# Quarter sums on GpSimd, a second gate and up block by seven products, and later tables, in a decoder trunk

## The chip, the cores and the metric

The kernel runs on one core of one Trainium2 chip. The metric is the device time of one execution in microseconds (us). Engines are named as in the profile: PE is TensorE (matmul), DVE is VectorE, ACT is ScalarE, POOL is GpSimd, SP is SyncE, which issues the weight DMAs.

## The reference

Two layers on a residual stream h of 256 tokens by 1024 channels, then an RMSNorm. All in float32:

```
for each layer:
  h = h + 1/2 * SwiGLU(RMSNorm(h))     # ffn1: gate and up 1024 x 2816, down 2816 x 1024
  u = RMSNorm(h); z = u @ W_in         # 5536 columns
  m = sum of three gated branches (latent attention, differential attention with ALiBi, trailing means)
  h = h + m @ W_out
  h = h + 1/2 * SwiGLU(RMSNorm(h))     # ffn2, same shapes
out = RMSNorm(h)
SwiGLU(x) = (silu(x @ W_gate) * (x @ W_up)) @ W_down
```

The change touches the four feed-forward stages (ffn1 and ffn2 of both layers) and the tables that attention reads: distances, mask, cosines and sines of the positions, and lambda.

## The kernel before, in words

**Products in three.** A float32 product is made of three matmuls. Each weight tile of 4 x 128 rows by 512 columns (1 MB, 128 partitions x 2048) is loaded by SP into a buffer `raw` (six of them), ACT casts it to `hi`, DVE subtracts `lo = raw - hi` (`wsplit_now` L182, `parts` L217; three buffers each of hi and lo), and PE adds hi*hi, hi*lo and lo*hi. For 256 tokens (two groups of 128) a tile is 24 matmuls of 512 columns.

**A feed-forward stage** (`ffn`, L492) goes over the 2816 columns in five blocks of 512 and a half block of 256. A block needs gate and up columns, 1024 by 1024 weights, four tiles. After a block, silu and a product make g, and in the next block PE transposes g and ACT and DVE split it into `ghi` and `glo` (`turned`). The down projection then has 22 groups of 128 rows in two halves of 512 columns.

**Seven products.** The fourth block (`SEVEN = 1536`) and the first eight row groups of the down projection are made as a two by two block product with seven instead of eight block products (Strassen and Winograd's scheme). Class `Seven` (L225) has these parts:

- `stream` (L235): sums of quarters of the activations: uf = hi + lo (2048 columns), four sums `sf` of 512 columns, then the split into `sh` (ACT) and `sl` (DVE).
- `sums` (L251): three of the four sums of weight quarters, 2048 columns each (t1 = b12 - b11, t2 = b22 - t1, b12 = b22 - b12). They stand at the start of the block before.
- `more` (L262): the splits p1 and p5, at the end of the block before.
- `run` (L280): products and splits in the order p1, p5, p2, p6, p3, p4, p7. The fourth sum, t1 = b21 - t2 (L297), overwrites t1 once p5 has been split from it. Each product is 12 matmuls.

`Down` (L317) does the same for the down projection. `open` makes the sums b11 - b12 and b22 - b12, `rest` (L345) two more, b22 - b11 and then that less b21, all by `minus` (L328, the subtraction itself is L329). Its products are mixed with ordinary tiles (`tiles`, L331).

**Buffers.** The large tiles (8 KB per partition) come from two sets: seven buffers of `big` (activations hi and lo, sh, sl, t2, ghi, gates and so on) and three of `big2` (uf, sf, t1, glo). A tile waits until one is free.

**Order.** Instructions are written in program order, and a scheduler gives each engine its own order by readiness in a cost model; waits follow from the tiles' reads and writes. On the chip each engine runs its list in order. `ahead()` (L175) begins the split of the first tile of the next block.

**Tables.** In layer 0, `table_loads` (L600) is called from the list `opening` (L1053), which is worked off between the first tiles: three small loads into `pi` and parts of a large tile `tables`. `tables()` (L611) is called at the start of the second block as `midway`.

Of the kernel before, what the change touches and what calls it, by code (L numbers as in the profile page):

```python
# [11 lines left out]
F32 = mybir.dt.float32  # L12
F32R = mybir.dt.float32r
I32 = mybir.dt.int32
BF16 = mybir.dt.bfloat16
AF = mybir.ActivationFunctionType
ALU = mybir.AluOpType
# [17 lines left out]

SEVEN = 1536

# [13 lines left out]
def plan():  # L51

    tiles = []

    def add(name, layer, k, nk, c, nc_):
        tiles.append((name, layer, k, nk, c, nc_))

    def ffn(layer, pre):
        for c in range(0, 2 * DFF, 1024):
            blocks = range(c, min(c + 1024, 2 * DFF), 512)  # L60
            order = [(b, k) for k in (0, 4) for b in blocks] if c == 0 else [(b, k) for b in blocks for k in (0, 4)]
            if c // 2 == SEVEN:
                order = [(c, 0), (c + 512, 0), (c + 512, 4), (c, 4)]
            for b, k in order:
                add(f"{pre}_gu", layer, k, 4, b, 512)
        for half in range(2):
            for k in range(0, KF, 4):
                add(f"{pre}_w_down", layer, k, min(4, KF - k), half * 512, 512)

    for l in range(DEPTH):  # L70
        ffn(l, "ffn1")
        for c, n in ((C_CQ, 416), (C_P, 512), (C_DQ, 512)):
            for k in (0, 4):
                add("w_in", l, k, 4, c, n)
        add("mla_w_uq", l, 0, 2, 0, 768)
        add("ukv", l, 0, 1, 0, 1024)
        for c in (C_DK, C_DV):
            for k in (0, 4):
                add("w_in", l, k, 4, c, 512)
        add("pool", l, 0, 4, 0, 128)  # L80
        for half in range(2):
            for i in range(3):
                for k in (0, 4):
                    add("w_in", l, k, 4, C_G + i * D + half * 512, 512)
        for half in range(2):
            for i in (2, 0, 1):
                add(f"w_branch{i}", l, 0, 4, half * 512, 512)
        for half in range(2):
            for k in (0, 4):
                add("w_out", l, k, 4, half * 512, 512)  # L90
        ffn(l, "ffn2")
    return tiles
# [3 lines left out]
def trunk(ctx, tc, x, xt, positions, wall, small, lamrow, fnorm, out):  # L96
# [128 lines left out]
    class Seven:  # L225
# [9 lines left out]
        def stream(self, uh, ul, place=big2):  # L235

            uf = big2([P, KD, S], F32, "uf")
            f = lambda a: a.rearrange("p k s -> p (k s)")
            nc.vector.tensor_tensor(out=f(uf), in0=f(uh).bitcast(F32), in1=f(ul).bitcast(F32), op=ALU.add)
            sf = place([P, 4, 4, P], F32, "sf")  # L240
            a = lambda i, j: uf[:, 4 * j:4 * j + 4, i * P:(i + 1) * P]
            for dst, x, y, op in ((0, a(1, 0), a(1, 1), ALU.add), (1, sf[:, 0], a(0, 0), ALU.subtract),
                                  (2, a(0, 0), a(1, 0), ALU.subtract), (3, a(0, 1), sf[:, 1], ALU.subtract)):
                nc.vector.tensor_tensor(out=sf[:, dst], in0=x, in1=y, op=op)
            self.sh = big([P, 4, 4, P], F32R, "sh")
            self.sl = big([P, 4, 4, P], F32R, "sl")
            g = lambda x: x.rearrange("p s k q -> p (s k q)")
            nc.scalar.copy(out=g(self.sh), in_=g(sf))
            nc.vector.tensor_tensor(out=g(self.sl), in0=g(sf), in1=g(self.sh).bitcast(F32), op=ALU.subtract)

        def sums(self, specs):  # L251

            s11, s12, s22, self.s21 = specs
            self.b12, self.b11, self.b22 = wraw(s12), wraw(s11), wraw(s22)
            self.t1 = big2([P, 4, 512], F32, "t1")
            self.t2 = big([P, 4, 512], F32, "t2")
            sub = lambda o, x, y: nc.vector.tensor_tensor(out=flat(o), in0=flat(x), in1=flat(y), op=ALU.subtract)
            sub(self.t1, self.b12, self.b11)
            sub(self.t2, self.b22, self.t1)
            sub(self.b12, self.b22, self.b12)  # L260
# [19 lines left out]
        def run(self, between):  # L280
# [15 lines left out]

            nc.vector.tensor_tensor(out=flat(self.t1), in0=flat(self.b21), in1=flat(self.t2), op=ALU.subtract)  # L297
            p3 = parts(self.b22)
# [18 lines left out]
    class Down(Seven):  # L317
# [10 lines left out]
        def minus(self, o, x, y):  # L328
            nc.vector.tensor_tensor(out=flat(o), in0=flat(x), in1=flat(y), op=ALU.subtract)  # L329

# [13 lines left out]

        def rest(self, ah, al, early):  # L345
            self.ah, self.al = ah, al
# [8 lines left out]
            early()  # L355
            self.tiles(0, [8])
            p5 = parts(self.b11)
            self.product(d, 0, p5)
# [3 lines left out]
            self.tiles(1, [8])  # L362
            b21 = wraw(self.spec(0, 4))
            p2 = parts(b21)
            self.product(a, (0, 1), p2, True)
            self.tiles(0, [12])
# [15 lines left out]
            add(u3, b, m1)  # L382
            add(m5, u3, m5)
            self.tiles(0, [20])
            for t, half, x in ((1, 0, u3), (0, 1, u2), (1, 1, m5)):
# [106 lines left out]
    def ffn(l, pre, u, following, midway=None):  # L492
# [19 lines left out]
        for c in range(0, DFF, 512):  # L512
            n = min(512, DFF - c)
            if c == 512 and midway:
                midway()
            spec = lambda b, k: (f"{pre}_gu", l, k, 4, b, 512)
            if c == 0:
# [13 lines left out]
                u.factor()  # L531
                seven = Seven(u.xh, u.xl)
                down = Down(lambda k: ghi[0][:, k, :], lambda k: glo[0][:, k, :])
            elif c == SEVEN:
                rows = seven.run(lambda: turned(*pending))
                ps = [[rows[t][m] for t in range(2)] for m in range(2)]
            elif n == 512:
                ps = []
                if c + 512 == SEVEN:
                    at = 2 * c + 1024  # L540
# [3 lines left out]
                for m in range(2):  # L544
                    ps.append(gemm_tokens([spec(2 * c + m * 512, k) for k in (0, 4)], u.xh, u.xl, 512))
                    if m == 0:
                        turned(*pending)
                        if c + 1024 == SEVEN:
                            seven.stream(u.hi, u.lo)
                        elif c == 2048:  # L550
                            down.stream(ghi[0], glo[0], big)
            else:
                both = gemm_tokens([spec(2 * c, k) for k in (0, 4)], u.xh, u.xl, 512, lambda: turned(*pending))
                ps = [[b[:, m * n:(m + 1) * n] for b in both] for m in range(2)]
            if c + 512 == SEVEN:
                seven.more()
            elif n < 512:
                down.open(lambda half, k: (f"{pre}_w_down", l, k, min(4, KF - k), half * 512, 512))
            elif c != SEVEN:
                ahead()  # L560
# [9 lines left out]
        nxt = following() if following else None  # L570
        down.rest(lambda k: ghi[k // 8][:, k % 8, :], lambda k: glo[k // 8][:, k % 8, :], lambda: turned(*pending))
        for half in range(2):
# [27 lines left out]
    def table_loads(after):  # L600

        tb["pi"] = pi = sp.tile([P, 2], I32, tag="pi", name="pi", bufs=1)
        tb["all"] = big([P, 8, S], F32, "tables")
        pr, lr = tb["all"][:, 4, :].bitcast(I32), tb["all"][:, 5, :]
        for dst in (pi, pr[:, :2], lr[:, :2].bitcast(I32)):
# [5 lines left out]
    def tables():  # L611
        pi, pr = tb["pi"], tb["all"][:, 4, :].bitcast(I32)

        part = tb["all"][:, 0:4, :].rearrange("p (t i) s -> p t i s", t=2)
        ci = sp.tile([P, 2, 2], I32, tag="ci", name="ci", bufs=1)
# [7 lines left out]
        for t in range(2):  # L623
            nc.vector.tensor_scalar(out=part[:, t, 0, :], in0=rf[:, 0, :], scalar1=cf[:, 0, t:t + 1], scalar2=4096.0,
                                    op0=ALU.subtract, op1=ALU.mult)
            nc.vector.tensor_scalar(out=part[:, t, 1, :], in0=rf[:, 1, :], scalar1=cf[:, 1, t:t + 1], scalar2=None,
                                    op0=ALU.subtract)
            nc.vector.tensor_tensor(out=part[:, t, 0, :], in0=part[:, t, 0, :], in1=part[:, t, 1, :], op=ALU.add)
            nc.vector.scalar_tensor_tensor(out=ndist[:, t, :], in0=part[:, t, 0, :], scalar=-1.0, in1=part[:, t, 0, :],
                                           op0=ALU.mult, op1=ALU.min)  # L630
            nc.gpsimd.affine_select(out=ndist[:, t, :], in_=ndist[:, t, :], compare_op=ALU.is_ge, fill=-1e33,
# [28 lines left out]

        lr = tb["all"][:, 5, :].rearrange("p (l f d) -> p l f d", l=DEPTH, f=4)
        lpr = tp.tile([P, DEPTH, 2, 32], F32, tag="C", name="lpr")
# [389 lines left out]
    opening += [lambda k=k: u.first(k) for k in range(4, KD)]  # L1052
    opening += [lambda: table_loads(u.hi[:, KD - 1, :2].bitcast(F32))] + [lambda: None] * 3  # L1053
    opening += [lambda t=t, n=n: nc.sync.dma_start(out=h[:, t, n * 512:(n + 1) * 512],
# [68 lines left out]
```

## Time and profile before

| what | value |
|---|---|
| median of 3 runs | 1208.63 us (1207.67 to 1209.4) |
| the profiled execution | 1207.28 us, span 1205.5 us |
| granted TensorE clock in it | 0.998 |
| ACT busy | 637.7 us, 53% of the span |
| SP weight loads of 1 MB | 182, median 4.9 us to landing |
| HBM read | 210.85 MB, 176 GB/s over the span |

A row of instructions names the line of the kernel, the engine, the operation, the tile written and the tiles read, the shape and the count, then busy time, the mean of one in ns, and the idle time in front of it with what ended it. A row of the timeline has the start, the duration, and in brackets the idle time before. A row of waits has the total, the number and the longest. A row of stretches has the length, then the busy time of each engine. A busy PE is not PE at its peak, since its matmuls overlap.

### The profile page before, as it was taken

The numbers are of one execution on the slowest core, as the hardware profiler recorded it, in microseconds if no ns is written. First come the engines' busy times: TensorE is split into PE (matmuls) and PEld (weight loads), VectorE is DVE, ScalarE is ACT, GpSimd is POOL, SyncE is SP. The second block draws the span as 40 slices with busy tenths as digits, with TensorE's granted clock in tenths as the row PEclk, the third lists the DMA queues.
The fourth block names the chain that finished last, engine by engine and source line by source line (L and its number), as shares of the span: only waits on it lengthen the run. The fifth ranks groups of instructions, "written<-read, shape, count | busy, mean of one in ns | idle before, by whom it ended". The sixth has DMA issues, their size and how long they took to land.

```text
span 1205.5 us, 14989 instructions
## 1 busy us (share of the span) xinstructions
PE 1186.7 (98%) x5896; PEld 991.4 (82%) x5896; DVE 923.0 (77%) x1200; ACT 637.7 (53%) x817; POOL 66.2 (5%) x127
## 2 busy tenths in 40 slices
PE   9989999999999999999999999999999999999997
PEld 7778888998788888888888888899977888888886
DVE  6889867777756757998757998768686486499876
ACT  5647446456544454655554655455465435546543
POOL 0000000700100000000000000025010000000000
PEclk9999999999999999999999999999999999999999
DMA  8846356336345454563764563653443554545540
GB/s 268 337 141 220 133 195 242 123 105 210 107 173 190 162 178 172 176 240 105 247 219 162 175 244 105 226 189 116 157 150 126 196 178 172 202 153 203 166 165 36
DMA packets 35478, 212.86 MB, mean 177 GB/s; under 512 B 4176, under 2 KB 5584, under 8 KB 12112
## 3 DMA queue, kind: packets, MB, share of 16 engines
q1 hardware_dynamic: 34272, 210.52, 50.2%
q10 hardware_dynamic: 1136, 1.40, 0.4%
q8 instruction: 46, 0.75, 0.2%
q14 instruction: 24, 0.20, 0.1%
HBM read 210.85 MB, written 1.05 MB: 176 GB/s over the span
## 4 chain that ended last, share of the span: by engine, by line
PE 88%; DVE 6%; issue 2%; ACT 2%; DMA 2%; POOL 0%; SPq 0%; POOLq 0%; ACTq 0%; DVEq 0%
PE acc L211 17%; PE acc L212 17%; PE acc L213 17%; PE acc L277 13%; PE acc L343 9%; PE e L343 3%; PE o L856 2%; DVE lo L194 2%; PE tr L502 1%; DMA raw<-wall 1%; PE tr L822 1%; PE tr L849 1%; PE tr L212 1%; PE tr L213 1%; PE tr L211 1%
## 5 line engine op out<-in xcount | busy, mean ns | idle before, releaser
L194 DVE TENSOR_TENSOR lo<-raw,hi 128x1024 fp32r<-128x1024 f32 (+3 forms) x258 | 392.1, 1535 | 151.5 <-ACT hi L193 150.8
L193 ACT CAST hi<-raw 128x1024 fp32r<-128x1024 f32 (+3 forms) x258 | 327.7, 1295 | 267.1 <-PE acc L213 135.9
L212 PE MATMUL acc<-lo,uhi 128*128 128x512 f32 (+1 forms) x768 | 300.0, 391 | 6.3 <-DVE lo L194 6.2
L211 PE MATMUL acc<-hi,uhi 128*128 128x512 f32 (+1 forms) x768 | 301.0, 393 | 0.9 <-DVE uhi L450 0.9
L213 PE MATMUL acc<-hi,ulo 128*128 128x512 f32 (+1 forms) x768 | 299.2, 390 | 0.9 <-DVE ulo L451 0.5
L212 PEld LDWEIGHTS acc<-lo,uhi 128*128 128x128 f32 x768 | 144.7, 188 | 36.5 <-DVE lo L194 8.1
L211 PEld LDWEIGHTS acc<-hi,uhi 128*128 128x128 f32 x768 | 144.3, 188 | 31.1 <-issue 2.6
L213 PEld LDWEIGHTS acc<-hi,ulo 128*128 128x128 f32 x768 | 144.6, 188 | 30.7 <-DVE ulo L451 1.1
L222 DVE TENSOR_TENSOR lo<-raw,hi 128x2048 fp32r<-128x2048 f32 x44 | 100.8, 2290 | 44.1 <-ACT hi L221 44.1
L221 ACT CAST hi<-raw 128x2048 fp32r<-128x2048 f32 x44 | 84.3, 1915 | 93.9 <-PE acc L213 36.1
L841 ACT ACTIVATE e<-e,mx 128x128 f32<-128x128 f32 (+1 forms) x96 | 42.7, 446 | 56.0 <-DVE mx L837 34.1
L343 PE MATMUL acc<-hi,ghi 128*128 128x512 f32 x168 | 66.3, 395 | 0.0
L343 PE MATMUL acc<-lo,ghi 128*128 128x512 f32 x168 | 65.7, 391 | 0.0
L343 PE MATMUL acc<-hi,glo 128*128 128x512 f32 x168 | 65.5, 391 | 0.0
L211 PE MATMUL acc<-uhi,hi 128*128 128x256 f32 x192 | 55.6, 290 | 0.0
L212 PE MATMUL acc<-ulo,hi 128*128 128x256 f32 x192 | 55.2, 288 | 0.0
L213 PE MATMUL acc<-uhi,lo 128*128 128x256 f32 x192 | 55.0, 288 | 0.0
L277 PE MATMUL acc<-hi,sl 128*128 128x512 f32 x128 | 49.8, 389 | 0.0
L277 PE MATMUL acc<-hi,sh 128*128 128x512 f32 x128 | 49.8, 389 | 0.0
L277 PE MATMUL acc<-lo,sh 128*128 128x512 f32 x128 | 49.8, 389 | 0.0
L416 POOL TENSOR_TENSOR r<-r,mhalf 128x2 f32<-128x2 f32 x6 | 4.2, 702 | 714.3 <-DVE r L415 714.3
L565 ACT ACTIVATE sg<-acc,r 128x512 f32<-128x512 f32 (+1 forms) x44 | 28.5, 653 | 27.7 <-PE acc L213 27.7
(258 smaller groups left out, 1968.2 us busy)
## 6 DMA issues: line engine op xcount, KB each, us to landing
raw<-wall SPq DMA_DIRECT2D x182, 1024.0 KB, 4.9
raw<-wall SPq DMA_DIRECT2D x26, 256.0 KB, 5.1
raw<-wall SPq DMA_DIRECT2D x10, 512.0 KB, 3.6
raw<-wall SPq DMA_DIRECT2D x4, 832.0 KB, 4.4
raw<-wall SPq DMA_DIRECT2D x2, 768.0 KB, 6.6
xT<-xt SPq DMA_DIRECT2D x8, 128.0 KB, 4.4
h<-x SPq DMA_DIRECT2D x4, 256.0 KB, 6.0
fn<-fnorm ACTq DMA_DIRECT2D x1, 512.0 KB, 4.2
```

The lines of the kernel that those rows point to most:

```text
L193: nc.scalar.copy(out=hif[:, ks], in_=rawf[:, ks])
L194: nc.vector.tensor_tensor(out=lof[:, ks], in0=rawf[:, ks], in1=hif[:, ks].bitcast(F32), op=ALU.subtract)
L211: nc.tensor.matmul(ps, lhsT=lh, rhs=rh, start=start, stop=False)
L212: nc.tensor.matmul(ps, lhsT=lh, rhs=rl, start=False, stop=False)
L213: nc.tensor.matmul(ps, lhsT=ll, rhs=rh, start=False, stop=stop)
L221: nc.scalar.copy(out=flat(hi), in_=flat(x))
L222: nc.vector.tensor_tensor(out=flat(lo), in0=flat(x), in1=flat(hi).bitcast(F32), op=ALU.subtract)
L277: nc.tensor.matmul(ps, lhsT=x, rhs=y, start=not onto and k == 0 and n == 0, stop=k == 3 and n == 2, skip_group_check=onto)
L343: nc.tensor.matmul(bank, lhsT=x, rhs=y, start=new and n == 0, stop=n == 2, skip_group_check=not new)
L565: nc.scalar.activation(out=sg, in_=ps[0][t], func=AF.Silu, scale=r)
L841: nc.scalar.activation(out=e[:, sl], in_=e[:, sl], func=AF.Exp, bias=mx[:, i:i + 1], scale=-(2.0 ** -(hd + 1)) if slope else -1.0, accum_o ...
L856: nc.tensor.matmul(o[:, hd * 64:(hd + 1) * 64], lhsT=eT[:, j * P:(j + 1) * P], rhs=v[:, kt, hd * 64:(hd + 1) * 64], start=(kt == 0), stop= ...
```

## The change

- All quarter sums go from DVE to POOL: uf and sf in `stream`, three in `sums`, the fourth in `run`, and `minus` in the down projection. The splits (`sl`, `lo`) stay on DVE.
- Two blocks of a stage are made by seven products, the third (column 1024) and the fifth (2048), in place of the fourth. The order of their weight tiles in memory follows. `stream` runs once, after the first block, and serves both.
- The down projection's `stream` moves from the fifth block to the start of the half block.
- In `rest`, b21's load, the split p2 and its product come ahead of p5.
- `table_loads` moves from the opening to the start of the third block of the first stage, with small tiles of its own; `tables()` moves into that stage's down projection, ahead of its last tile of the first half. A large tile is no longer needed for them.

```
-SEVEN = 1536
+SEVENS = 1024, 2048
...
-            if c // 2 == SEVEN:
+            if c // 2 in SEVENS:
                 order = [(c, 0), (c + 512, 0), (c + 512, 4), (c, 4)]
...
-            nc.vector.tensor_tensor(out=f(uf), in0=f(uh).bitcast(F32), in1=f(ul).bitcast(F32), op=ALU.add)
+            nc.gpsimd.tensor_tensor(out=f(uf), in0=f(uh).bitcast(F32), in1=f(ul).bitcast(F32), op=ALU.add)
...
-                nc.vector.tensor_tensor(out=sf[:, dst], in0=x, in1=y, op=op)
+                nc.gpsimd.tensor_tensor(out=sf[:, dst], in0=x, in1=y, op=op)
...
-            sub = lambda o, x, y: nc.vector.tensor_tensor(out=flat(o), in0=flat(x), in1=flat(y), op=ALU.subtract)
+            sub = lambda o, x, y: nc.gpsimd.tensor_tensor(out=flat(o), in0=flat(x), in1=flat(y), op=ALU.subtract)
...
-            nc.vector.tensor_tensor(out=flat(self.t1), in0=flat(self.b21), in1=flat(self.t2), op=ALU.subtract)
+            nc.gpsimd.tensor_tensor(out=flat(self.t1), in0=flat(self.b21), in1=flat(self.t2), op=ALU.subtract)
...
         def minus(self, o, x, y):
-            nc.vector.tensor_tensor(out=flat(o), in0=flat(x), in1=flat(y), op=ALU.subtract)
+            nc.gpsimd.tensor_tensor(out=flat(o), in0=flat(x), in1=flat(y), op=ALU.subtract)
...
-        def rest(self, ah, al, early):
+        def rest(self, ah, al, early, late):
...
             self.tiles(0, [8])
+            b21 = wraw(self.spec(0, 4))
+            p2 = parts(b21)
+            self.product(a, (0, 1), p2, True)
             p5 = parts(self.b11)
...
             self.tiles(1, [8])
-            b21 = wraw(self.spec(0, 4))
-            p2 = parts(b21)
-            self.product(a, (0, 1), p2, True)
             self.tiles(0, [12])
...
             add(m5, u3, m5)
+            late()
             self.tiles(0, [20])
...
-            if c == 512 and midway:
-                midway()
+            if c == 1024 and midway:
+                table_loads(g[0][:, :2])
...
                 seven = Seven(u.xh, u.xl)
+                seven.stream(u.hi, u.lo)
...
-                        if c + 1024 == SEVEN:
-                            seven.stream(u.hi, u.lo)
-                        elif c == 2048:
-                            down.stream(ghi[0], glo[0], big)
             else:
+                down.stream(ghi[0], glo[0], big)
                 both = gemm_tokens([spec(2 * c, k) for k in (0, 4)], u.xh, u.xl, 512, lambda: turned(*pending))
...
-        tb["all"] = big([P, 8, S], F32, "tables")
-        pr, lr = tb["all"][:, 4, :].bitcast(I32), tb["all"][:, 5, :]
+        tb["pr"] = pr = sp.tile([P, S], I32, tag="pr", name="pr", bufs=1)
+        tb["lr"] = lr = sp.tile([P, DEPTH * P], F32, tag="lr", name="lr", bufs=1)
...
-    opening += [lambda: table_loads(u.hi[:, KD - 1, :2].bitcast(F32))] + [lambda: None] * 3
+    opening += [lambda: None] * 4
```

`tables()` computes the same values, with its partial distances in `ndist` and a small tile instead of the large one.

More of the change, by code (lines that the diff above doesn't have):

```diff
@@ L532, in ffn @@
                 seven = Seven(u.xh, u.xl)
+                seven.stream(u.hi, u.lo)
                 down = Down(lambda k: ghi[0][:, k, :], lambda k: glo[0][:, k, :])
-            elif c == SEVEN:
+            elif c in SEVENS:
                 rows = seven.run(lambda: turned(*pending))
@@ L538, in ffn @@
                 ps = []
-                if c + 512 == SEVEN:
+                if c + 512 in SEVENS:
                     at = 2 * c + 1024
@@ L547, in ffn @@
                         turned(*pending)
-                        if c + 1024 == SEVEN:
-                            seven.stream(u.hi, u.lo)
-                        elif c == 2048:
-                            down.stream(ghi[0], glo[0], big)
             else:
+                down.stream(ghi[0], glo[0], big)
                 both = gemm_tokens([spec(2 * c, k) for k in (0, 4)], u.xh, u.xl, 512, lambda: turned(*pending))
                 ps = [[b[:, m * n:(m + 1) * n] for b in both] for m in range(2)]
-            if c + 512 == SEVEN:
+            if c + 512 in SEVENS:
                 seven.more()
@@ L558, in ffn @@
                 down.open(lambda half, k: (f"{pre}_w_down", l, k, min(4, KF - k), half * 512, 512))
-            elif c != SEVEN:
+            elif c not in SEVENS:
                 ahead()
@@ L570, in ffn @@
         nxt = following() if following else None
-        down.rest(lambda k: ghi[k // 8][:, k % 8, :], lambda k: glo[k // 8][:, k % 8, :], lambda: turned(*pending))
+        down.rest(lambda k: ghi[k // 8][:, k % 8, :], lambda k: glo[k // 8][:, k % 8, :], lambda: turned(*pending),
+                  midway or (lambda: None))
         for half in range(2):
@@ L611, in tables @@
     def tables():
-        pi, pr = tb["pi"], tb["all"][:, 4, :].bitcast(I32)
-        part = tb["all"][:, 0:4, :].rearrange("p (t i) s -> p t i s", t=2)
+        pi, pr = tb["pi"], tb["pr"]
         ci = sp.tile([P, 2, 2], I32, tag="ci", name="ci", bufs=1)
@@ L623, in tables @@
         for t in range(2):
-            nc.vector.tensor_scalar(out=part[:, t, 0, :], in0=rf[:, 0, :], scalar1=cf[:, 0, t:t + 1], scalar2=4096.0,
+            nd, part = ndist[:, t, :], tp.tile([P, S], F32, tag="C", name="part")
+            nc.vector.tensor_scalar(out=nd, in0=rf[:, 0, :], scalar1=cf[:, 0, t:t + 1], scalar2=4096.0,
                                     op0=ALU.subtract, op1=ALU.mult)
[L626 to L630, printed above, removed]
+            nc.vector.tensor_scalar(out=part, in0=rf[:, 1, :], scalar1=cf[:, 1, t:t + 1], scalar2=None, op0=ALU.subtract)
+            nc.vector.tensor_tensor(out=nd, in0=nd, in1=part, op=ALU.add)
+            nc.vector.scalar_tensor_tensor(out=nd, in0=nd, scalar=-1.0, in1=nd, op0=ALU.mult, op1=ALU.min)
             nc.gpsimd.affine_select(out=ndist[:, t, :], in_=ndist[:, t, :], compare_op=ALU.is_ge, fill=-1e33,
@@ L659, in tables @@
         nc.vector.tensor_scalar(out=cosq, in0=cosk, scalar1=MLA_SCALE, scalar2=None, op0=ALU.mult)
-        lr = tb["all"][:, 5, :].rearrange("p (l f d) -> p l f d", l=DEPTH, f=4)
+        lr = tb["lr"].rearrange("p (l f d) -> p l f d", l=DEPTH, f=4)
         lpr = tp.tile([P, DEPTH, 2, 32], F32, tag="C", name="lpr")
```

## Prediction

> **What bounds the kernel now.** I read the page first, then the waits of TensorE (PE), then the chain.
>
> ```profile
> span 1205.5 us, 14989 instructions
> PE 1186.7 (98%) x5896; PEld 991.4 (82%) x5896; DVE 923.0 (77%) x1200; ACT 637.7 (53%) x817; POOL 66.2 (5%) x127
> PE 88%; DVE 6%; issue 2%; ACT 2%; DMA 2%; POOL 0%; SPq 0%; POOLq 0%; ACTq 0%; DVEq 0%
> ```
> ```profile
> PE acc L212 <- DVE lo L194: 6.2, 3, 3.7
> ```
> ```profile
> 139.00 2.72 PE acc L277 x12
> 164.28 2.72 PE acc L277 x12
> 175.16 5.44 PE acc L343 x24
> ```
>
> PE carries 88% of the chain and loses almost nothing to anyone: its largest wait, for the subtraction that makes the low part of a split weight tile, is 6.2 us in all. The chain also gives the true price of a matmul of 512 columns: 12 follow each other in 2.72 us, so 0.227 us each (the 0.39 us of a single one overlaps its neighbours). A kernel in this state gets faster if PE issues fewer matmuls and the others keep up. So the second question is how near VectorE (DVE) is to not keeping up. I cut one steady feed-forward stage, the second of layer 0, into stretches:
>
> ```profile
> core 0: us, PE busy (x) PEld busy (x) DVE busy (x) ACT busy (x) POOL busy (x), PEclk, DMA share, GB/s
> 449.30:471.10 21.80, 21.80 (x102) 18.12 (x101) 15.42 (x14) 9.90 (x8) 0.00 (x0) 1.00 0.57 193
> 471.10:494.80 23.70, 23.70 (x110) 19.74 (x109) 23.08 (x15) 11.72 (x9) 0.00 (x0) 1.00 0.51 175
> 494.80:514.75 19.95, 19.95 (x93) 16.60 (x93) 19.11 (x14) 15.95 (x12) 0.00 (x0) 1.00 0.47 153
> 514.75:537.50 22.75, 22.75 (x106) 18.90 (x106) 22.08 (x19) 12.42 (x11) 0.00 (x0) 1.00 0.71 244
> 537.50:560.80 23.30, 23.30 (x109) 19.18 (x108) 19.74 (x14) 12.27 (x11) 0.00 (x0) 1.00 0.28 92
> 560.80:608.00 47.20, 47.20 (x213) 38.78 (x213) 33.85 (x26) 24.65 (x21) 0.00 (x0) 1.00 0.68 241
> ```
>
> These are the second gate and up block, the third, the fourth by seven products (the run), the fifth, the half block with the head of the down projection, and the rest. PE is busy without a gap. DVE is full in the third to the fifth: 19.11 of 19.95 us in the run. DVE keeps up with very little room. In the run the room per tile is small as well:
>
> ```profile
> 494.83 1.92 ACT L221 CAST hi<-raw 128x2048 fp32r<-128x2048 f32 x1 [3.52 <-PE acc L213]
> 503.69 2.29 DVE L222 TENSOR_TENSOR lo<-raw,hi 128x2048 fp32r<-128x2048 f32 x1 [0.20 <-ACT hi L221]
> ```
>
> A split may begin when PE has finished with the tile three before it (three buffers; the cast waits for PE). It takes 1.92 + 2.29 = 4.2 us, and PE has two products, 5.44 us, to do meanwhile. The slack is 1.2 us.
>
> **The change part by part.** *Fewer matmuls.* A block by four tiles is 96 matmuls, by seven products 84. One more such block per stage saves 12 x 0.227 = 2.72 us, in four stages 10.9 us, all on the path.
>
> *Work off DVE.* One stage of before:
>
> ```profile
> L329 DVE TENSOR_TENSOR raw<-raw 128x2048 f32<-128x2048 f32 x4 | 9.2, 2290 | 0.1
> L257 DVE TENSOR_TENSOR t<-raw,t 128x2048 f32<-128x2048 f32 x1 | 2.3, 2289 | 0.0
> L239 DVE TENSOR_TENSOR uf<-ghi,glo 128x2048 f32<-128x2048 f32 x1 | 2.3, 2281 | 0.0
> L297 DVE TENSOR_TENSOR t<-raw,t 128x2048 f32<-128x2048 f32 x1 | 2.3, 2282 | 0.0
> L244 DVE TENSOR_TENSOR sf<-uf 128x512 f32<-128x512 f32 x4 | 2.6, 686 | 0.0
> L486 DVE TENSOR_TENSOR glo<-tr,ghi 128x512 fp32r<-128x512 f32 x11 | 7.1, 684 | 0.0
> L282 DVE TENSOR_TENSOR u<-acc,m 128x512 f32<-128x512 f32 x1 | 0.7, 682 | 0.0
> ```
>
> Four L329, three L257 and one L297 are 8 x 2.29 = 18.3 us; two streams of one L239 and four L244 (0.69 us) are 10.1 us. DVE loses 28.4 us per stage and gains, for the second seven-product block, three splits (6.9) and five additions of 0.68 (3.4). Taken alone that is 18 us of relief.
>
> *The same work on GpSimd (POOL).* There it is 12 sums of 2048 columns (four per seven-product run, four in the down projection) and two streams. The trace has no POOL subtraction of that size; its own subtractions and additions bound it:
>
> ```profile
> 230.48 0.60 POOL L910 TENSOR_TENSOR pp<-pp 128x254 f32<-128x254 f32 x1
> 231.05 0.22 POOL L916 TENSOR_TENSOR pp<-pp 128x16 f32<-128x16 f32 x1
> 231.23 0.70 POOL L918 TENSOR_TENSOR pp<-pp 128x240 f32<-128x240 f32 x1
> 342.29 1.05 POOL L962 TENSOR_TENSOR o<-o,hs 128x512 f32<-128x512 f32 x1
> ```
>
> From L916 to L918, both subtractions, a column costs 0.48/224 = 2.14 ns, so 2048 columns about 4.55 us; from L916 to the addition L910 1.6 ns, so 3.45 us. I take 4.55, since the sums are subtractions, and 1.05 for a quarter of a stream (L962 has its size). A stage then has 12 x 4.55 + 2 x (4.55 + 4.2) = 72 us on POOL, of some 180. [...]
>
> *What POOL takes from DVE.* Two engines are free beside each other only if nothing is shared. These rows show that something is:
>
> ```profile
> 220.03 1.37 DVE L194 TENSOR_TENSOR lo<-raw,hi 128x1024 fp32r<-128x1024 f32 x1 [3.49 <-ACT hi L193]
> 221.99 1.21 DVE L194 TENSOR_TENSOR lo<-raw,hi 128x1024 fp32r<-128x1024 f32 x1
> 234.45 1.22 DVE L194 TENSOR_TENSOR lo<-raw,hi 128x1024 fp32r<-128x1024 f32 x1
> 342.60 2.96 DVE L194 TENSOR_TENSOR lo<-raw,hi 128x1024 fp32r<-128x1024 f32 x2 [2.11 <-ACT hi L193]
> ```
> ```profile
> 220.28 1.69 POOL L918 TENSOR_TENSOR pp<-pp 128x240 f32<-128x240 f32 x1
> 222.18 1.49 POOL L910 TENSOR_TENSOR pp<-pp 128x254 f32<-128x254 f32 x1
> ```
>
> POOL's L918 takes 1.69 instead of 0.70 when it begins behind a DVE split that ends at 221.40, and L910 1.49 instead of 0.60 beside the split of 221.99 to 223.20: each ends about 0.5 us after that split. The other way round, the two splits at 342.60 take 2.96 where two in a row take about 2.3, with the first 0.74 us inside POOL's L962. So a DVE subtraction with both inputs in SBUF and a POOL instruction exclude each other, and whoever comes second waits for the end of the other. No row shows it for a POOL instruction above 1.05 us at work. [...]
>
> *The sum by stretches.* I add what DVE keeps and what POOL holds, take off two thirds of DVE's operations that read PSUM (one SBUF input at most, so they can run beside POOL when the queue has them in front), and compare with PE's time.
>
> The run: DVE 19.11 - 2.28 (L297) = 16.83. POOL surely has the run's own sum, which must wait for a split of the same buffer, and one more that becomes ready there (in the third block the next block's first sum, as its weight buffers come free; in the fifth the down projection's uf, as a buffer comes free): 9.1. Covered: two glo, two u, two g of about 0.68, 4.1, two thirds 2.7. 16.83 + 9.1 - 2.7 - 19.95 = 3.3 us of stall, twice per stage.
>
> The fourth block in the new order is a plain one: DVE 22.08 less uf, sf (5.0) and sl (2.3), that is 14.8, and two sums 9.1: 23.9, less cover below 22.75. No stall. The two blocks in front of the third (45.5 us) hold DVE 38.5 - 5.0 - 6.9 = 26.6 and three sums, 13.7: no stall.
>
> The half block and the head of the down projection: DVE 19.74 - 3 x 2.29 + sl 2.29 + the split of p2, now in front of p5, 2.29 = 17.45; POOL four quarters of the stream (4.2) and two sums (9.1); cover two thirds of 3.4. 17.45 + 13.3 - 2.3 = 28.4 against 23.3 + 2.72 (p2's product is moved in) = 26.0: 2.4 us. The rest, without one sum and the split of p2: 33.85 - 4.6 + 9.1 = 38.4 against 47.2 - 2.7 = 44.5, nothing.
>
> A stage loses 3.3 + 3.3 + 2.4 = 9.0 and saves 2.7: +6.3, four stages +25.2. Without any cover it is 6.0 + 6.0 + 4.7 - 2.7 = +14.0, in all +56; with full cover and 3.45 us per sum nothing is lost.
>
> *Tables.* The opening loses time to them:
>
> ```profile
> 33.79 0.17 DVE L659 TENSOR_SCALAR cosq<-cosk 128x32 f32<-128x32 f32 x1
> 38.27 7.09 DVE L194 TENSOR_TENSOR lo<-raw,hi 128x512 fp32r<-128x512 f32 x6
> 29.04 0.72 POOL L416 TENSOR_TENSOR r<-r,mhalf 128x2 f32<-128x2 f32 x1 [12.60 <-DVE r L415]
> ```
> ```profile
> 39.00 0.50 PE L212 MATMUL acc<-lo,uhi 128*128 128x512 f32 x1 [2.31 <-DVE lo L194]
> ```
>
> PE waited 2.31 us for a split that stood behind the table steps; with these in the down projection, whose rest has 6 us of room, that wait goes. But the first stream now stands right behind the first block: up to 8.8 us of POOL work beside splits that come just in time, and the instruction that makes r (29.04) queues behind it on POOL, the activations behind r. Between 0 and 8.8; I take 1, as most of the stream fits before r is due. Net -1.3. The three small loads move from the opening to the third block on ACT's queue, 0.4 us each, hidden by ACT's idle half. PE order in the down projection changes, the count doesn't.
>
> Sum against the profiled execution (1207.28 us): 1207.28 + 25.2 - 1.3 = 1231.2. The median of before is 1.35 us above that execution, so 1232.5; I say 1232.
>
> **The rivals.** *Faster: POOL finds room.* If POOL's sums start in idle DVE time or give way in pieces, PE keeps its 2.72 us per stage and the opening its 2.31: 1207.28 - 10.9 - 2.3 + 1.35 = 1195. For it: 18 us less on DVE per stage, and POOL instructions start early since POOL has nothing else. Against it: DVE's row of the run, and the 1.2 us of slack per tile. The point of decision is 2.7 us of stall per stage, a little over half of one sum. Chance 0.25; between the two, stall about equal to gain and within 0.2% (2.4 us, about what a measurement of this kernel can tell from no change), 0.07.
>
> *Slower still: queues.* Engines run in order. ACT's sh waits for all of a stream:
>
> ```profile
> 57.08 1.91 ACT L248 CAST sh<-sf 128x2048 fp32r<-128x2048 f32 x1 [7.39 <-DVE sf L244]
> ```
>
> Here it cost ACT 7.39 us idle and PE nothing. On POOL a stream takes 4.55 + 4.2 and can be stopped by three splits, 6.9 us more. Where sh, or a third sum, falls into a run, casts queue behind it and PE loses up to that 6.9 once per stage: 28 us, 1260. Chance 0.18.
>
> **How the numbers follow.** Forecast 0.50, heavier 0.18, faster 0.25, same 0.07: slower 0.68. The range reaches from the faster case, 1195, to just over the heavier one, 1262 (without cover the forecast ends at 1264), and leaves out about one in five.
>
> **What would show it.** Right: PE idle of about 9 us per stage inside the two runs and at the head of the down projection, released by DVE lo L222 and L194; splits of 2048 columns whose mean is well above 2290 ns; POOL sums of 4.5 us and, where they wait, about 6.8. Wrong: splits still at 2290 ns beside POOL sums (nothing shared), or sums near 3.4 us, or PE without gaps in the runs; then the time is near 1195. If the gap before sh on ACT holds back casts, the second rival was at work.

## The result and the profile after

The changed kernel takes 1366.95 us (median of 4 runs, 1365.85 to 1367.57) against 1208.15 us (4 runs): ratio 1.1314, 95% interval 1.1296 to 1.1332. It is slower, as forecast, but by 158.8 us and not by 24: far outside the stated range.

The page of the kernel after, with its busy times, two rows of its slices and the chain:

```profile
span 1364.1 us, 15023 instructions
PE 1227.0 (90%) x5848; PEld 1010.5 (74%) x5848; DVE 1027.9 (75%) x1160; ACT 660.3 (48%) x834; POOL 439.7 (32%) x215
PE   7859789999999979897997797999999999779788
POOL 3461560420000084264154517206000004461640
PE 54%; DVE 18%; issue 10%; POOL 7%; ACT 5%; DMA 0%; POOLq 0%; ACTq 0%; DVEq 0%
```

Of the 16 slices in which PE is below 9, 15 have POOL at 2 tenths or more, and of the 13 in which POOL has 0, PE is at 9 in 12 (these are the mixing parts, where POOL has few sums to make). PE carries 54% of the chain instead of 88%. DVE has 28 us of sums less per stage and yet 105 us more busy time. The groups by shape say where that comes from (count, busy time, mean of one in ns):

```profile
L194 DVE TENSOR_TENSOR lo<-raw,hi 128x2048 fp32r<-128x2048 f32 x74 | 230.9, 3128 | 45.0 <-ACT hi L193 44.7
L222 DVE TENSOR_TENSOR lo<-raw,hi 128x2048 fp32r<-128x2048 f32 x60 | 183.9, 3065 | 54.9 <-ACT hi L221 54.8
L222 DVE TENSOR_TENSOR lo<-t,hi 128x2048 fp32r<-128x2048 f32 x24 | 81.3, 3387 | 21.6 <-ACT hi L221 21.6
L194 DVE TENSOR_TENSOR lo<-raw,hi 128x1024 fp32r<-128x1024 f32 x128 | 155.3, 1234 | 66.6 <-ACT hi L193 66.5
```

A split of 2048 columns, 2290 ns before (L222), has a mean of 3065 to 3387; 158 of them take 496.1 us instead of 158 x 2.29 = 361.8, 134 more. The splits of 1024 columns, in the mixing parts without POOL sums, keep their 1.23 us.

The second stage of layer 0 in time order, first POOL, then DVE:

```profile
486.89 1.28 POOL L244 TENSOR_TENSOR sf<-sf,uf 128x512 f32<-128x512 f32 x1
488.14 4.59 POOL L257 TENSOR_TENSOR t<-raw 128x2048 f32<-128x2048 f32 x1
492.70 1.29 POOL L244 TENSOR_TENSOR sf<-uf,sf 128x512 f32<-128x512 f32 x1
...
524.23 5.46 POOL L257 TENSOR_TENSOR t<-raw 128x2048 f32<-128x2048 f32 x1 [19.18 <-DMA raw<-wall]
529.65 6.65 POOL L297 TENSOR_TENSOR t<-raw,t 128x2048 f32<-128x2048 f32 x1
541.56 4.77 POOL L257 TENSOR_TENSOR t<-raw,t 128x2048 f32<-128x2048 f32 x1 [5.26 <-DMA raw<-wall]
546.29 6.61 POOL L257 TENSOR_TENSOR raw<-raw 128x2048 f32<-128x2048 f32 x1
```
```profile
495.96 4.71 DVE L249 TENSOR_TENSOR sl<-sf,sh 128x2048 fp32r<-128x2048 f32 x1 [10.18 <-ACT sh L248]
500.60 6.60 DVE L194 TENSOR_TENSOR lo<-raw,hi 128x2048 fp32r<-128x2048 f32 x1
...
531.77 6.68 DVE L222 TENSOR_TENSOR lo<-t,hi 128x2048 fp32r<-128x2048 f32 x1
...
541.76 6.71 DVE L222 TENSOR_TENSOR lo<-t,hi 128x2048 fp32r<-128x2048 f32 x1
549.00 6.04 DVE L222 TENSOR_TENSOR lo<-raw,hi 128x2048 fp32r<-128x2048 f32 x1
```

A split of 6.7 us is 2.29 of work behind 4.4 of waiting for a POOL sum, and POOL's 6.65 is 4.6 of its own work behind the rest of a split. The third block's run lasts from 526.21 to 559.31; three POOL sums begin in it and a fourth (524.23) just before it. At the start of the stage another thing is seen: the last quarter of the stream (492.70) stands behind a weight sum on POOL, `sh` waits for it on ACT, `sl` for that on DVE with 10.18 us of idle time, and the split of 500.60 stands behind `sl`.

What this does to PE is a row of the waits and one view of stretches (length, busy PE, PEld, DVE, ACT, POOL, then PEclk, the granted clock):

```profile
PE acc L277 <- DVE lo L222: 46.8, 14, 12.2
PE acc L212 <- DVE lo L194: 27.0, 8, 7.8
```
```profile
500.90:511.10 10.20, 3.84 (x9) 3.07 (x10) 10.20 (x5) 2.99 (x2) 4.15 (x1) 0.50 0.29 92
511.10:538.40 27.30, 24.55 (x116) 20.12 (x115) 19.07 (x10) 15.82 (x15) 12.07 (x2) 1.00 0.38 127
538.40:541.80 3.40, 3.30 (x8) 2.65 (x9) 3.40 (x5) 0.42 (x1) 0.24 (x1) 0.51 0.62 260
548.70:552.10 3.40, 3.40 (x9) 2.63 (x10) 3.40 (x2) 0.00 (x0) 3.40 (x1) 0.50 0.00 0
```

In this stage PE has half the clock for 10.2 us from 500.90 on, in and behind the second of two stops of 3.9 and 6.9 us, and for 3.4 us behind each of its six other stops above 2 us (2.4 to 4.7 us). In the chain of this stage a matmul just after the stop takes 0.43 us, a little later 0.23:

```profile
508.05 0.43 PE acc L213
...
512.52 0.23 PE acc L211
```

The length of a stop alone does not decide this. The same stop of PE in the first stage, with a wait of 3.7 us, has no half clock behind it in the kernel before and has one in the run with one GpSimd sum further down (first row before, second that run; the 0.50 is the clock):

```profile
66.30:73.10 6.80, 4.21 (x18) 3.49 (x19) 6.80 (x6) 0.75 (x2) 0.00 (x0) 1.00 0.43 152
66.30:73.05 6.75, 5.64 (x13) 4.46 (x14) 6.66 (x5) 0.54 (x1) 0.00 (x0) 0.50 0.63 193
```

The largest single stop of the changed kernel, with a wait of 12.2 us in the third block of the first stage, has another beginning: the tables. POOL, then DVE, then PE, and last one of the DVE rows again in the first run below, where POOL has no sums:

```profile
82.10 4.53 POOL L257 TENSOR_TENSOR t<-raw,t 128x2048 f32<-128x2048 f32 x1 [0.31 <-DMA pi<-positions]
86.57 4.50 POOL L257 TENSOR_TENSOR raw<-raw 128x2048 f32<-128x2048 f32 x1
```
```profile
82.11 4.54 DVE L619 TENSOR_SCALAR ci<-pi 128x2 int32<-128x2 int32 x1 [5.12 <-DMA pi<-positions]
86.63 4.47 DVE L636 CAST pf<-pi 128x2 f32<-128x2 int32 x1
```
```profile
94.92 0.79 PE L277 MATMUL acc<-lo,sh 128*128 128x512 f32 x1 [12.19 <-DVE lo L222]
```
```profile
97.52 0.16 DVE L619 TENSOR_SCALAR ci<-pi 128x2 int32<-128x2 int32 x1
```

`tables()` is called in the down projection, but the scheduler put its first steps into DVE's queue here, in front of a weight split. They wait 5.12 us for the positions, whose load starts only when POOL has made its small copies behind a sum; then two steps of 0.16 us take 4.5 each beside two POOL sums. These steps read one tensor of two columns, so the waiting is not confined to subtractions of two tensors.

An account of the whole kernel from the trace: the intervals between the starts of successive matmuls above 0.62 us, less 0.23 each, add up to 9.6 us before and 133.8 after; the intervals from 0.25 to 0.62 us in stretches at half clock, less 0.228 each, add up to 1.6 and 40.3. So +124.2 of stops, +38.7 of slow issue, -10.9 of matmuls left out: +152.0 of the 158.6 by which the span grew. (Single stops in the text below are whole intervals, with the 0.23.)

### The profile page after: what moved, and what is told of

It reads as the page before. It is cut to its first block, busy times and chain, and to the rows that moved or that the text cites. A ratio compares the mean times of both kernels' runs of the same rounds, so it can differ in the third digit from the quotient of the medians.

```text
span 1364.1 us, 15023 instructions
## 1 busy us (share of the span) xinstructions
PE 1227.0 (90%) x5848; PEld 1010.5 (74%) x5848; DVE 1027.9 (75%) x1160; ACT 660.3 (48%) x834; POOL 439.7 (32%) x215
## 4 chain that ended last, share of the span: by engine, by line
PE 54%; DVE 18%; issue 10%; POOL 7%; ACT 5%; DMA 0%; POOLq 0%; ACTq 0%; DVEq 0%
PE acc L211 11%; PE acc L212 11%; PE acc L213 11%; PE acc L343 8%; DVE lo L194 6%; DVE lo L222 6%; PE acc L277 5%; POOL sf L244 5%; PE e L343 2%; POOL uf L239 2%; ACT hi L193 2%; PE o L854 2%; DVE glo L487 1%; PE tr L820 1%; ACT hi L221 1%
## 5 line engine op out<-in xcount | busy, mean ns | idle before, releaser
L194 DVE TENSOR_TENSOR lo<-raw,hi 128x1024 fp32r<-128x1024 f32 (+4 forms) x242 | 429.4, 1793 | 124.4 <-ACT hi L193 123.9
L193 ACT CAST hi<-raw 128x1024 fp32r<-128x1024 f32 (+4 forms) x242 | 296.3, 1253 | 260.9 <-PE acc L213 74.1
L212 PE MATMUL acc<-lo,uhi 128*128 128x512 f32 (+1 forms) x640 | 256.3, 401 | 27.0 <-DVE lo L194 27.0
L211 PE MATMUL acc<-hi,uhi 128*128 128x512 f32 (+1 forms) x640 | 256.9, 402 | 11.3 <-ACT hi L193 10.4
L213 PE MATMUL acc<-hi,ulo 128*128 128x512 f32 (+1 forms) x640 | 254.0, 397 | 0.4 <-DVE ulo L442 0.4
L222 DVE TENSOR_TENSOR lo<-raw,hi 128x2048 fp32r<-128x2048 f32 x60 | 183.9, 3065 | 54.9 <-ACT hi L221 54.8
L277 PE MATMUL acc<-lo,sh 128*128 128x512 f32 x192 | 82.6, 430 | 38.8 <-DVE lo L222 38.7
L329 POOL TENSOR_TENSOR raw<-raw 128x2048 f32<-128x2048 f32 x16 | 83.1, 5195 | 77.4 <-DVE lo L222 77.1
L222 DVE TENSOR_TENSOR lo<-t,hi 128x2048 fp32r<-128x2048 f32 x24 | 81.3, 3387 | 21.6 <-ACT hi L221 21.6
L297 POOL TENSOR_TENSOR t<-raw,t 128x2048 f32<-128x2048 f32 x8 | 43.1, 5384 | 141.7 <-DVE lo L222 141.7
L277 PEld LDWEIGHTS acc<-lo,sh 128*128 128x128 f32 x192 | 39.7, 207 | 52.3 <-DVE lo L222 43.9
```

What stands on the lines that cost most here:

```text
L193: nc.scalar.copy(out=hif[:, ks], in_=rawf[:, ks])
L194: nc.vector.tensor_tensor(out=lof[:, ks], in0=rawf[:, ks], in1=hif[:, ks].bitcast(F32), op=ALU.subtract)
L211: nc.tensor.matmul(ps, lhsT=lh, rhs=rh, start=start, stop=False)
L212: nc.tensor.matmul(ps, lhsT=lh, rhs=rl, start=False, stop=False)
L213: nc.tensor.matmul(ps, lhsT=ll, rhs=rh, start=False, stop=stop)
L222: nc.vector.tensor_tensor(out=flat(lo), in0=flat(x), in1=flat(hi).bitcast(F32), op=ALU.subtract)
```

## The experiments

SBUF is the memory in which the tiles lie, PSUM the one that PE writes its sums to. Theory A: a POOL sum and a DVE subtraction of two SBUF inputs exclude each other for a whole instruction, so splits wait and PE runs dry. Theory B: sums come late for those who need them (4.5 us where DVE took 2.3). Theory C: two seven-product blocks per stage are more than ACT and DVE can split for, wherever the sums are made. Times are medians; before was 1208.0 to 1209.2 us beside these runs.

**All sums back on VectorE.** The changed kernel, and in its five places:

```
-nc.gpsimd.tensor_tensor(...)
+nc.vector.tensor_tensor(...)
```

> The changed kernel with every quarter sum back on VectorE: two seven-product blocks, the new order and the late tables stay. Theory A (a GpSimd sum and a VectorE subtraction of two SBUF inputs exclude each other for the whole instruction, so splits wait and TensorE runs dry): the loss goes, 1190 to 1215 us, splits of 2048 columns back at 2290 ns. Theory B (the loss comes from sums being late for those who need them, 4.5 us instead of 2.3): also 1190 to 1215. Theory C (seven splits in 19 us twice per stage are too much for ScalarE and VectorE, wherever the sums are made): still above 1300.

Measured: 1245.78 us, ratio 1.0311 (1.0293 to 1.0328). 121 us of the loss are gone, and splits are back at 2289 ns, but 38 remain: neither A or B (1190 to 1215) nor C (above 1300). By the account above, 88 of the 121 are stops and 28 slow issue. Of the remainder, two thirds of the second stage's stops (6.0 of 8.8 us) lie in the stretch of the half block and the head of the down projection, where DVE's own load fills the time (DVE, the third engine in the row, is busy for all of its 24.00 us):

```profile
550.00:574.00 24.00, 18.79 (x75) 14.02 (x74) 24.00 (x20) 11.13 (x11) 0.00 (x0) 0.87 0.27 91
```

The small sums of the stream that the kernel before made in its plain fifth block now fall here, beside two weight sums, five tile splits and `sl`. Stops and slow issue of the whole kernel come to 45.6 + 12.2 us.

**The kernel before with its sums on GpSimd,** the reverse edit there:

> The kernel before with the sums on GpSimd and nothing else changed: one seven-product block, tables early. A: most of the loss is here, 1280 to 1340 us, since 8 sums and 2 streams per stage still meet the splits. B: also a loss, about 1250 to 1300, with VectorE splits near 2290 ns. C: within 15 us of before, 1208 to 1223.

Measured: 1252.97 us, ratio 1.0371 (1.0347 to 1.0395). That is less than A's number and inside B's, but B wanted the splits near 2290 ns, and they are stretched:

```profile
L194 DVE TENSOR_TENSOR lo<-raw,hi 128x2048 fp32r<-128x2048 f32 x90 | 297.0, 3309 | 66.0 <-ACT hi L193 65.7
```

So the sums on GpSimd cost 45 by themselves, the rest of the change 38 (the second block, the moved stream, the new order in `rest` and the tables, which were not run apart except for the tables), and all together 159. More than the sum of the two is plausible if they use up the same slack, and a second block brings four more sums per stage; neither was tried by itself.

**GpSimd work for nobody.** Sums on VectorE as in the first run, and beside each:

```
+    def ghost(x, n=4):
+        four = lambda a: a.rearrange("p (o q) -> p o q", o=1).broadcast_to([P, 4, P])
+        nc.gpsimd.tensor_copy(out=scr[:, :2], in_=x[:, :2])
+        for i in range(n):
+            nc.gpsimd.tensor_tensor(out=scr.rearrange("p (o q) -> p o q", o=4), in0=four(ones), in1=four(ident), op=ALU.subtract)
```

> The kernel of the first run, sums on VectorE, with idle GpSimd work beside it: for each sum of 2048 columns, and for each stream's four small sums together, GpSimd makes four subtractions of 512 columns of constants into a scratch tile that nobody reads, started by a copy of two columns of the sum's input. Nobody waits for the result. A: splits are stretched all the same and the time rises over the first run by 30 us or more. B: within 5 us of the first run. C: within 5 us of the first run.

Measured: 1393.55 us, 148 us above the same kernel without it. The groups of POOL and of DVE in it:

```profile
L134 POOL TENSOR_TENSOR scr<-ones,ident 128x512 f32<-128x512 f32 x256 | 625.3, 2443 | 20.0
```
```profile
L202 DVE TENSOR_TENSOR lo<-raw,hi 128x2048 fp32r<-128x2048 f32 x74 | 195.6, 2655 | 14.9 <-ACT hi L201 14.7
L230 DVE TENSOR_TENSOR lo<-raw,hi 128x2048 fp32r<-128x2048 f32 x60 | 165.3, 2760 | 42.0 <-ACT hi L229 41.9
```

No sum comes from POOL here, and the splits are stretched all the same. B cannot explain that. The 148 us are not the size of the effect in the changed kernel, since POOL is busy for 776 us here and for 440 there.

**The same, writing only.** In place of each subtraction:

```
+            nc.gpsimd.memset(scr, 0.0)
+            nc.gpsimd.memset(scr, 1.0)
```

> The run with idle GpSimd work beside sums on VectorE, but each subtraction of 512 columns into the scratch tile replaced by two memsets of it, so GpSimd is busy and writes about as long without reading. If a GpSimd instruction excludes VectorE by its reads: within 10 us of the run without it (1246). If any GpSimd instruction does: 1330 or above, as with the subtractions (1394).

Measured: 1247.79 us, 2 us above the run without it:

```profile
L133 POOL MEMSET scr<- 128x512 f32 x256 | 135.2, 528 | 14.8
L134 POOL MEMSET scr<- 128x512 f32 x256 | 135.1, 528 | 14.6
```
```profile
L202 DVE TENSOR_TENSOR lo<-raw,hi 128x2048 fp32r<-128x2048 f32 x74 | 168.3, 2286 | 28.1 <-ACT hi L201 28.1
```

POOL is busy for 450 us of this run, about as long as in the changed kernel (440), with the same small copies as in the run before, and a split takes 2286 ns. So of these two kinds of GpSimd work it is the one that reads that holds up the splits (2655 to 2760 ns beside the subtractions).

**Sums in four pieces.** The changed kernel with

```
+    def pieces(o, x, y, op=ALU.subtract):
+        for i in range(0, 2048, 512):
+            nc.gpsimd.tensor_tensor(out=o[:, i:i + 512], in0=x[:, i:i + 512], in1=y[:, i:i + 512], op=op)
```

> The changed kernel with each GpSimd sum of 2048 columns cut into four of 512. A: a split waits for one piece of about 1.2 us and not for 4.5, and gets in between; mean of the splits of 2048 columns falls from 3.1 to 2.5 to 2.8 us and the time from 1367 to 1240 to 1310. B: the sums end no earlier (four overheads more), so 1360 or above.

Measured: 1306.11 us, 61 us less than whole sums, splits at a mean of 2491 to 2861 ns. Beside whole sums, in the changed kernel, the means are 3065 to 3387. This fits a split that waits for one instruction of POOL, so that shorter ones cost less. B expected no gain.

**Streams on VectorE, weight sums on GpSimd:**

> The changed kernel with the two streams of a stage (uf and four small sums each) on VectorE and the weight sums on GpSimd. A: GpSimd holds 55 us per stage in place of 72, and the subtraction that makes sl no longer stands in front of tile splits while it waits for a stream: 1300 to 1340 us, the long stops of the second block gone. If the streams were the whole of it (order of the queues and not the exclusion): near the run with all sums on VectorE, 1246 us.

Measured: 1320.68 us, 46 us less than the changed kernel. In the second stage the stop of 3.9 us ahead of 500.35 has no counterpart; one of 6.6 in the second block and three of 3.0 to 3.3 in the first run remain. So, taken off in this order, the streams are 46 of the 121 us, with the queue order that they cause, and the weight sums 75, with the tables' stop (13.0 us in this run). The other order was not run.

**Only the down projection's stream on GpSimd,** on top of the first run, with uf in four pieces on both engines:

> The kernel with two seven-product blocks and sums on VectorE (1246 us), and only the down projection's stream on GpSimd, its uf in four pieces. This moves 5 us per stage from VectorE at the head of the down projection, where that run has its largest stops. A: pieces of 1.2 us hold up the splits of the fifth block's end and the half block, so little is won, 1235 to 1265. If VectorE's own load is all that counts there: 1215 to 1235.

Measured: 1265.12 us, 19 us more than the first run, although DVE is full there and gives up 5 us per stage. The time is just past A's upper end, and the trace shows more than A said (PE's waits, then DVE and the splits):

```profile
PE tr L506 <- DVE g L569: 38.8, 8, 9.3
```
```profile
564.27 2.29 DVE L252 TENSOR_TENSOR sl<-sf,sh 128x2048 fp32r<-128x2048 f32 x1 [6.47 <-ACT sh L251]
L194 DVE TENSOR_TENSOR lo<-raw,hi 128x2048 fp32r<-128x2048 f32 x74 | 174.9, 2372 | 16.8 <-ACT hi L193 16.8
```

The splits are hardly longer on average (2372 ns). The stop of 9.3 us, one per stage, is for g, which stands in DVE's queue behind `sl`; `sl` waits for the stream, which takes POOL 16.9 us here (545.45 to 562.31) beside the splits. Lateness, theory B, is at work as well, with the exclusion making POOL late.

**One GpSimd sum per run.** The kernel before with L297 alone on GpSimd:

> The kernel before with only the run's fourth sum on GpSimd, one GpSimd sum per stage. Theory A: VectorE gives up 2.28 us and a split waits up to 4.55, a net delay of 2.3 us in the run, of which about 1 is taken by the slack: 1208 to 1220 us, one split per run at 4.5 to 6.8 us. If the sums cost only where they are late: 1207 to 1210 with every split at 2290 ns.

Measured: 1208.56 us, ratio 0.9996 (0.9986 to 1.0006): no difference. The trace shows why; POOL, then DVE:

```profile
494.88 4.63 POOL L297 TENSOR_TENSOR t<-raw,t 128x2048 f32<-128x2048 f32 x1 [59.92 <-DVE lo L222]
```
```profile
494.72 0.74 DVE L567 SCALAR_TENSOR_TENSOR g<-acc,r,sg 128x512 f32<-128x512 f32 x1
496.00 0.75 DVE L567 SCALAR_TENSOR_TENSOR g<-acc,r,sg 128x512 f32<-128x512 f32 x1 [0.54 <-PE acc L213]
497.95 3.72 DVE L222 TENSOR_TENSOR lo<-raw,hi 128x2048 fp32r<-128x2048 f32 x1 [1.20 <-ACT hi L221]
```

The sum begins while DVE reads PSUM and waits for ACT, so it delays the split by 1.4 us, and DVE has 2.28 us less to do. Both expectations held the time; the long split that A named did not come. A sum in a good place is free; the three that begin in the third block's run of the changed kernel are not.

**The run's sum three times over on VectorE,** before with a loop of three around L297, nothing on GpSimd:

> The kernel before with the run's fourth sum (t1 = b21 - t2) made three times over on VectorE, which is 4.57 us more of VectorE in each run and nothing on GpSimd. It prices a delay in the run by itself. With a stop of about 3.3 us per stage and TensorE at half clock for 3.4 us behind it: 1208 + 4 x 5 = 1228, half clock in the trace after each stop. Without a clock effect 1221. If the run had room after all: within 3 us of before.

Measured: 1221.14 us, +12.7, or 3.2 per stage. The second stage has stops of 1.1 and 1.8 us and no half clock behind them (the granted clock of the run is 0.994, that of the kernel before beside it 0.994 to 0.998). So 4.57 us of delay in the run cost 3.2, about as the slack of 1.2 had it, and these stops cost no clock. Short stops can: in the second stage of the first run, half clock for 6.8 us comes with five stops of 0.7 to 2.0 us within some 15 us.

**Late tables alone,** on the kernel before:

> The kernel before with the late tables alone: their loads at the third block, the tables themselves in the first stage's down projection, small tiles in place of the large one. All theories: the wait of 2.3 us at the second block of the first stage goes, 1202 to 1208 us.

Measured: 1203.36 us, ratio 0.9961 (0.9948 to 0.9974), so about 5 us are won. One stop of PE of any size was left, in the first stage:

```profile
PE acc L212 <- DVE lo L194: 3.9, 1, 3.9
```

**Late tables and later sums.** That stop stands behind two weight sums in DVE's queue. So, on top:

```
-                if c + 512 == SEVEN:
...
-                    seven.sums([spec(at, 0), spec(at + 512, 0), spec(at + 512, 4), spec(at, 4)])
...
                 for m in range(2):
                     ps.append(gemm_tokens([spec(2 * c + m * 512, k) for k in (0, 4)], u.xh, u.xl, 512))
                     if m == 0:
+                        if c + 512 == SEVEN:
...
+                            seven.sums([spec(at, 0), spec(at + 512, 0), spec(at + 512, 4), spec(at, 4)])
...
                         turned(*pending)
```

> The kernel before with the late tables, and with the three weight sums of the third block asked for after its first half and not at its start, so that VectorE has the tile splits in front of them. The run with late tables alone has one large stop left, 4.3 us in the first stage, at a tile whose split stood behind two sums. If the order in the queue is its cause, it goes: 1195 to 1201 us. If the sums then come too late for the run of seven products: 1205 or above.

Measured: 1197.2 us, ratio 0.9899 (0.9881 to 0.9917), faster than both kernels. The stops come to 2.3 us in all; the largest waits of PE are now

```profile
PE tr L139 <- DVE idle L134: 1.0, 1, 1.0
PE acc L211 <- DVE k L792: 1.0, 2, 0.5
```

## Why the prediction was right in direction and wrong in size

*Right.* A sum of 2048 columns takes POOL 4.5 to 4.6 us when nothing is in its way, as worked out (4.55). The exclusion, read from rows of 1 us and carried to whole sums as an estimate, holds at 4.6 us (a split of 6.68 us beside the sum of 529.65), and in the two runs with idle work it is one of reads (2655 to 2760 ns beside subtractions, 2286 beside memsets). Operations that read PSUM ran beside POOL, as the cover has it (u at 548.40 in 0.68 us beside the sum of 546.29, g in 0.74 and 0.75 in the run with one sum), but a single SBUF input did not spare the steps of two columns their 4.5 us. The two runs and the half block do stop PE. On the kernel before, the late tables win what was said and a little more (5 us, where the stop was put at 2.3).

The second stage, stretch by stretch (us, stops by the measure of the account):

| stretch | forecast | measured |
|---|---|---|
| the two blocks in front of the third | 0 | 10.3 |
| the third block's run | 3.3 | 8.0 |
| the fourth block | 0 | 0 |
| the fifth block's run | 3.3 | 3.2 |
| half block and head of the down projection | 2.4 | 5.3 |
| the rest | 0 | 3.1 |
| sum | 9.0 | 29.9 |

*The sum by stretches failed, and it failed first at "no stall" in front of the third block.* It set DVE's and POOL's time against the length of a stretch, as if both could be laid out freely. 26.6 + 13.7 us in 45.5 seemed to leave 5 us over, but the stream's 8.75 us on POOL, which fall into this stretch, were left out (they have a term of 1 us in the opening alone). With them it is 49 us in 45.5 before any cover. In the trace PE stops there for 3.9 and 6.9 us, and the other missing part is order. POOL put a weight sum in front of the last quarter of the stream, DVE stood idle for 10.18 us with `sl` at the head of its queue, and the tile split behind it then met another sum. That is the second rival's mechanism, which the prediction put into the runs and at 6.9 us. The run with streams on VectorE puts the streams at 46 us of the total, though a stop of 6.6 us stays in this stretch without them.

*The run: 3.3 us was forecast from two POOL sums.* The third block's run has three that begin in it, with stops of 3.2, 3.1 and 2.4 us. The first two are about what the slack of 1.2 us leaves of 4.5. With three sums in place of two the prediction's own sum gives 7.8 us, near the 8.0 measured, so here the count was wrong: all three sums of the fifth block became ready, not one. The fifth block's run has 3.2 as forecast, but from one sum (uf at 595.77) and not from two: its own sum (581.11) lies in a free place, as in the run with one sum. Cover is a matter of place, and the agreement of a mean of two thirds with both runs is luck at least in part.

*The tables in the down projection had "6 us of room".* Their first steps did not run there but in the third block's run of the first stage, behind a load that POOL's queue had made late and beside two POOL sums, and PE stopped for 12.6 us. That is most of why the first stage has 43.0 us of stops where each other has 29.9. The prediction saw only the loads' cost on ACT's queue.

*The clock had no term.* A prediction that adds stops also has to add what PE loses after them: 38.7 us of slow issue here.

*The two seven-product blocks were booked as a gain of 10.9 us plus relief for DVE.* With the sums on DVE they cost 38, together with the moved stream, the new order and the tables. The prediction never summed that case; its stretch of the half block, 17.45 us of DVE without any sums, would have had 17.45 + 6.9 + 5 = 29 us against 26.0.

The range left such a case out since every term in it was a mean over a stretch. The heavier rival, at 1260, had the mechanism in one place instead of in all of them. (The bound without cover, given as 1264, comes to 1263.)

Open: the 88 us of stops and 28 of slow issue in the 121 us are read from the traces; no run had stops of this length without the clock. The 38 us of the rest of the change were not taken apart.

## What to carry to other kernels

Moving a step to an idle engine was not free here, as the two engines held each other up (a split of 2.29 us took 6.7 beside a sum of 4.6): look in the trace for an instruction of each that overlap, and compare both with the same instruction alone. Where they exclude each other, count collisions in the order of the queues, one by one, and not busy time per stretch. Here the kernel took 61 us less with its sums in four pieces than with whole ones, and one sum in a place where the other engine reads PSUM and waits cost nothing (ratio 0.9996). A call's place in the program is not its place in an engine's queue: look where the scheduler put the steps (those of `tables()` began at 82.11 us, in the third block). In this kernel, whose TensorE hardly stops, two moves of order won 11 us, where fewer matmuls paid for on a full engine lost time.

## What the runs showed of the hardware

In the changed kernel a VectorE subtraction of two SBUF tensors waited for a whole GpSimd sum that reads SBUF (6.7 us instead of 2.29 beside a sum of 4.6); in the run with idle writes it did not wait for memsets, which only write (2286 ns beside 512 of them). In the changed kernel a cast and an integer step that read one tensor of two columns waited as well (4.5 us instead of 0.16), while an addition that reads PSUM kept its 0.68 us beside a GpSimd sum and, in the run with one sum, a product that reads PSUM its 0.75. In the second stage of the changed kernel TensorE's clock was halved for 3.4 us or more behind stops of 2.4 us and longer. It was not behind stops of 1.1 and 1.8 us in the second stage of the run with the repeated sum, nor behind one of 3.3 us in the changed kernel (at 861.17). What besides the length decides is not shown.
